# Layer B's fillers tied to earlier score products, doses by half pair, and the norm's broadcast behind its row copy

## The chip, the core and the metric

One core of one Trainium2 chip runs the whole program. Its engines work side by side, each through its own list of instructions in a fixed order: PE (TensorE) multiplies matrices, DVE (VectorE) and ACT (ScalarE) work on whole tiles and read what PE has written, POOL (GpSimd) works on tiles in the large on-chip memory, and SP issues most DMA transfers. The metric is the device time of one launch in microseconds (us), taken as the median of several runs; less is better.

## What is computed

A trunk of two decoder layers on one sequence of 512 positions with 1024 channels, in float32. Layer A is attention with compressed, selected and windowed branches, and is not touched here. Layer B reads shared keys and values through three groups of dilated windows, which are merged by their softmax sums, beside an attention over 256 memory rows. Each layer ends in a squared-ReLU MLP.

```python
DIL_PATTERNS = ((128, 1), (512, 4), (2048, 16))
...
for gi, (window, dil) in enumerate(DIL_PATTERNS):
    ...
    s = jnp.einsum('bhqd,bhqkd->bhqk', q_b[:, gi], k_g).astype(jnp.float32) * scale
    s = jnp.where(valid, s, NEG)
    lse = jax.nn.logsumexp(s, axis=-1, keepdims=True)
    p = jnp.exp(s - lse)
    outs.append(jnp.einsum('bhqk,bhqkd->bhqd', p.astype(v.dtype), v_g))
    lses.append(lse)
wts = jax.nn.softmax(jnp.stack(lses), axis=0).astype(v.dtype)
return jnp.sum(jnp.stack(outs) * wts, axis=0)
...
x = x + jnp.concatenate([o_main, o_mem], axis=-1) @ b_w_out[i]
x = x + squared_relu_mlp(rmsnorm(x, mlp_norm[layer]), w_up[layer], w_down[layer])
```

## The kernel before

The eight slots (heads) of layer B are taken in four *slot pairs*, sp = 0 to 3; the two slots of a pair lie in the two halves of the 128 partitions, so that their products use the two halves of the PE array side by side. The queries of pair 0 are projected before the attention begins. Everything else that PE has to do in this layer is *filler*: the query projections of pairs 1 to 3 (`proj_b`), that of the memory queries (`mem_q`), and the first part of the output projection (`outpart`). Each filler step is one `mm3` (lines 267 to 272): three products, high times high, high times low, low times high, which together stand for one product in float32.

`attn_b` makes eight items for a pair: two slots s, two window halves w (w = 0 is the near window, w = 1 the two dilated ones) and two halves ih of the query blocks. `scores` (products at line 762) runs once for both slots of an item pair and fills the two banks of the pool `ps`; one such call is called a *score group* here, and there are 16. `soft` masks the scores on DVE (line 737), takes exponentials on ACT (line 226) and, for w = 1, adds the two dilated groups on POOL (line 1635). The `back` of an item transposes the exponentials on PE (lines 1646 and 1655) and copies them on ACT (line 750); when all of a window half are there, `close0` or `close1` multiplies them with the values (line 754). `norm_b` then merges the two halves: sums are transposed and copied to rows (lines 1695 to 1701), a chain of small DVE steps makes the factors (lines 1706 to 1718, 307, 308), they are transposed again (line 1725) and copied to rows (line 1729), and two products spread them over the partitions (*the broadcast*, lines 1733 and 1738), which ACT (line 1735) and DVE (lines 1736, 1739) read. `norm_b` runs as a generator in `side`, one step per item; `NY` and `NZ` are the numbers of steps that it lets pass ahead of line 1725, and between the row copy and the broadcast.

`attend` emits fronts and backs of the items in turn, a back two items behind its front, and after each it lets `side` go one step and `work` (the fillers) as many as a dose says: `RB[seg]`, added up, where `seg` is the pair, or 4 for the memory items. The order in which the engines run this is then set by the framework's scheduler, which moves instructions of the emitted program forward on a modelled time line as far as their inputs, buffers and given dependences allow. `add_manual_dep` gives it a dependence that the data don't have.

PE's results go to banks: `acc` 2 (projections), `ps` 2 (scores), `po` 1 (products with values), and `pt` 2 with one more bank, `px`, that every third tile of `pt` gets. A tile can be written only when what was in its bank has been read. DX is the number of steps by which the transposes of pair 0's queries trail their projection.

Of the kernel before, what the change touches and what calls it, by code (L numbers as in the profile page):

```python
# [44 lines left out]


RA = (2.22, 1.29, 1.62, 1.96)
RB = (1.58, 1.85, 1.29, 2.4, 1.9)


RC = (6.5, 0.6, 0.7)

WK = 0.13
WB = (26, 0)
DX = 12


PA = 13
# [1 line left out]

DELAY = 5

NY, NZ = 6, 2

NW = 11
END, WAIT = object(), object()
# [26 lines left out]
class Work:  # L93


    def __init__(self):
        self.q, self.done = [], set()
# [29 lines left out]
class Item:  # L127


    def __init__(self, front, back, args, seg, need=None):  # L130
        self.front, self.back, self.args, self.seg, self.need = front, back, args, seg, need


def paced(gen, n):
# [4 lines left out]
        next(gen, None)  # L139


def attend(items, work, side, ratios, seen, lag=1):


    late, due = [], 0.0

    def tick(it):
        nonlocal due
        side.step()
        due += ratios[it.seg]  # L150
        while due >= 1.0:
            due -= 1.0
            if work.step() in (END, WAIT):
                due = 0.0

    def back(it):
        it.back(*it.args, it.res)
        tick(it)

    for it in items:  # L160
        if it.need:
            work.need(it.need)
        it.res = it.front(*it.args)
        seen.append(it.seg)
        tick(it)
        late.append(it)
        if len(late) > lag:
            back(late.pop(0))
    for it in late:
        back(it)  # L170
# [10 lines left out]
class K:  # L181
    def __init__(self, ctx, tc, ins, out):
        self.tc, self.nc, self.ins, self.out = tc, tc.nc, ins, out
        ps = lambda n, b: ctx.enter_context(tc.tile_pool(name=n, bufs=b, space=bass.MemoryType.PSUM))
        sb = lambda n, b: ctx.enter_context(tc.tile_pool(name=n, bufs=b))
        self.pacc, self.pS, self.pT, self.pO = ps("acc", 2), ps("ps", 2), ps("pt", 2), ps("po", 1)
        self.px, self.third, self.turns = ps("px", 1), self.pS, 0
        self.one = sb("one", 1)
        self.sb = sb("sb", 1)
        self.dram = ctx.enter_context(tc.tile_pool(name="dram", bufs=1, space=bass.MemoryType.DRAM))  # L190
        self.n = 0
        self.ev = 3
        self.staged = []
        self.sums, self.marks = {}, []
        self.adds, self.far = self.blocks(), 5
        self.lab = "s"

    BUFS = dict(
        act=12, st=3, w=4, qk=8, pt4=4, p2=6, raw=2, tmp=4, sq=1, rb=1, tq=2, qki=2, ki=2, x=8, r1=1, r2=1, r3=1, r4=2, r5=2, r6=3, r7=2, nm=6, su=5, cr=6, c1=2, c2=2, nb=4,
# [67 lines left out]
    def mm3(self, ps, lh, rh, start, stop, again=False):  # L267

        mm = self.nc.tensor.matmul
        mm(ps, lh[0], rh[0], start=start, stop=False, skip_group_check=again)  # L270
        mm(ps, lh[0], rh[1], start=False, stop=False, skip_group_check=again)  # L271
        mm(ps, lh[1], rh[0], start=False, stop=stop, skip_group_check=again)  # L272

# [478 lines left out]
    def pair(self, *a, **k):  # L752

        i = self.nc.tensor.matmul(*a, **k)  # L754
        self.tc.add_manual_dep(
            i.ins, self.turned.ins.name, mybir.DependencyInfo(mybir.DependencyClass.Sync, mybir.DependencyReason.DATA),
            reason="both halves of the array together",
        )

    def together(self, other, *a, **k):  # L760

# [671 lines left out]
    def layer_b(self):  # L1433
# [52 lines left out]
        items = []  # L1486
        for sp in range(4):
            items += self.attn_b(sp, pb[sp], kp[sp], oT, side)
        items += self.mem_items(self.kf1, qm, kk, om, 4, "mem")
        attend(items, work, side, RB, seen, 2)  # L1490
        while side.step() is not END or work.step() is not END:
            pass
        drain(self.outpart(oT + om, 3, 6, ins["w_bo"], None, 3, 3))
# [77 lines left out]
    def attn_b(self, sp, q4, kv, oT, side):  # L1571
# [8 lines left out]
        def scores(w, ih):  # L1580
# [6 lines left out]
            for ii in range(2):  # L1587
                i, n = 2 * ih + ii, sizes[ii]
                blk = slice(i * P, (i + 1) * P)
                for g in range(1 + w):  # L1590
                    for s in range(2):
# [10 lines left out]
                        else:  # L1602
# [2 lines left out]
                                start=True, stop=True,  # L1605
                            )
                o += n
            for s in range(2):
                made[s] = soft(s, w, ih, Sp[s], sizes)

# [74 lines left out]
            side.add(self.norm_b(st0, st1, acc[0], O, oT))  # L1685

        order = [(s, w, ih) for w in range(2) for ih in range(2) for s in range(2)]
        return [Item(front, back, a, sp, sp or None) for a in order]

    def norm_b(self, st0, st1, acc, O1, oT):  # L1690

# [179 lines left out]
```

## Time and profile before

| | us |
|---|---|
| median of three runs | 1251.24 |
| lowest and highest run | 1250.85, 1255.25 |
| the profiled execution | 1249.75 |
| its span, first to last instruction | 1248.0 |
| PE busy in the span | 1223.8 |
| weight loads of PE busy | 1000.9 |
| DVE, ACT, POOL busy | 817.5, 720.2, 336.5 |

The span is that of the profiled execution; 1.75 us of its time lie outside it. The granted clock is the share of its full rate that PE's clock had, and its mean is 0.997 over the span. A row of the view in order of time gives the start, the duration, the engine, the source line, the operation with its result and inputs, the number of instructions merged in it, and in brackets how long the engine stood idle before it and what ended that. Matmuls overlap, so a row's duration is longer than the time to the next start. One product in float32 is two instructions in the trace, so a row of the program's order with one product is x2 there.

### The profile page before, as it was taken

Reading aid. Unit: us, or ns where it says so; the run is one execution under the profiler, and the core shown is the slowest. Engines: PE = TensorE matmul, PEld = TensorE weight load, DVE = VectorE, ACT = ScalarE, POOL = GpSimd, SP = SyncE. Lnnn points to the kernel's source line nnn. Section 1 sums busy time; section 2 is a strip of 40 time slices with the busy share of each in tenths; the row PEclk is TensorE's granted clock in tenths of the full one; section 3 lists DMA queues with packets and bytes.
Section 4 is the critical chain, followed back from the end, with each engine's and each line's share of the span. In section 5 each row is a group of like instructions: output and inputs, shape, how many; then the busy total and the mean of one; then the engine's idle time right before and its main releaser. Section 6 shows DMA issues by size and latency. Waiting matters only on the chain.

```text
span 1248.0 us, 17996 instructions
## 1 busy us (share of the span) xinstructions
PE 1223.8 (98%) x6307; PEld 1000.9 (80%) x6307; DVE 817.5 (66%) x1533; ACT 720.2 (58%) x1579; POOL 336.5 (27%) x452
## 2 busy tenths in 40 slices
PE   9999999999999999999999999988999999999998
PEld 7768877787788888888888888876788888888887
DVE  6857576764567557475589466876767747557466
ACT  6834678873475454463657446666666445364462
POOL 4536874731040000000002786642131000000000
PEclk9999999999999999999999999999999999999999
DMA  7531232442498796896976431211469689697634
GB/s 269 202 105 46 99 105 93 95 118 77 127 287 236 228 271 217 271 245 204 293 206 184 129 96 60 70 39 29 123 193 301 206 269 248 204 290 226 171 106 164
DMA packets 62218, 215.34 MB, mean 173 GB/s; under 512 B 6928, under 2 KB 15312, under 8 KB 61616
## 3 DMA queue, kind: packets, MB, share of 16 engines
q1 hardware_dynamic: 50656, 143.69, 35.4%
q0 software_dynamic: 9728, 35.87, 14.8%
q10 hardware_dynamic: 1744, 34.63, 7.4%
q8 instruction: 50, 0.82, 0.3%
q14 instruction: 40, 0.33, 0.1%
HBM read 208.83 MB, written 72.35 MB: 225 GB/s over the span
## 4 chain that ended last, share of the span: by engine, by line
PE 78%; ACT 4%; DVE 2%; issue 1%; DMA 1%; POOL 1%; ACTq 0%; POOLq 0%; DVEq 0%
PE s_ps L270 13%; PE s_ps L271 13%; PE s_ps L272 13%; PE s_acc L270 6%; PE s_acc L271 6%; PE s_acc L272 6%; PE s_pt L271 3%; PE s_pt L272 3%; PE s_pt L270 3%; PE s_po L754 3%; ACT s_p L226 2%; PE s_ps L762 1%; DVE s_w L265 1%; ACT s_pt L750 1%; DMA s_st<-in_w_mem_dram 1%
## 5 line engine op out<-in xcount | busy, mean ns | idle before, releaser
L265 DVE TENSOR_TENSOR s_w<-s_st,s_w 128x1024 fp32r<-128x1024 f32 (+3 forms) x254 | 293.6, 1161 | 258.9 <-ACT s_w L263 253.5
L263 ACT ACTIVATE s_w<-s_st 128x1024 fp32r<-128x1024 f32 (+4 forms) x260 | 251.8, 971 | 216.3 <-PE s_pt L272 60.0
L270 PE MATMUL s_ps<-s_act,s_w 128*128 128x512 f32 x560 | 218.5, 392 | 0.4 <-DVE s_x L1189 0.3
L271 PE MATMUL s_ps<-s_act,s_w 128*128 128x512 f32 x560 | 218.4, 390 | 0.1
L272 PE MATMUL s_ps<-s_act,s_w 128*128 128x512 f32 x560 | 218.1, 390 | 0.0
L1210 POOL DMA_DIRECT2D sum<-sum x16 | 14.2, 888 | 432.6 <-ACT s_p L226 432.6
L271 PEld LDWEIGHTS s_ps<-s_act,s_w 128*128 128x128 f32 x560 | 105.2, 188 | 22.8 <-issue 0.8
L270 PEld LDWEIGHTS s_ps<-s_act,s_w 128*128 128x128 f32 x560 | 105.0, 188 | 22.9 <-DVE s_x L1189 0.8
L272 PEld LDWEIGHTS s_ps<-s_act,s_w 128*128 128x128 f32 x560 | 105.1, 188 | 21.6
L270 PE MATMUL s_acc<-s_w,s_act 128*128 128x512 f32 (+3 forms) x288 | 101.9, 359 | 1.4 <-ACT s_act L286 0.9
L271 PE MATMUL s_acc<-s_w,s_act 128*128 128x512 f32 (+3 forms) x288 | 101.6, 354 | 0.0
L272 PE MATMUL s_acc<-s_w,s_act 128*128 128x512 f32 (+3 forms) x288 | 100.3, 353 | 0.0
L226 ACT ACTIVATE s_p<-s_ps 128x512 f32<-128x512 f32 x64 | 38.1, 595 | 90.1 <-PE s_ps L272 87.4
L742 POOL TENSOR_SCALAR s_p<-s_p,s_cr,s_ab 128x128 f32<-128x128 f32 (+3 forms) x96 | 62.0, 672 | 58.6 <-DVE s_cr L1099 34.8
L226 ACT ACTIVATE s_p<-s_ps,s_nm 128x256 f32<-128x256 f32 (+3 forms) x128 | 65.7, 527 | 13.9 <-PE s_pt L1117 4.5
L750 ACT ACTIVATE s_pt<-s_pt 128x512 f32<-128x512 f32 (+2 forms) x99 | 51.4, 529 | 27.0 <-PE s_pt L1655 7.3
L270 PEld LDWEIGHTS s_acc<-s_w,s_act 128*128 128x128 f32 x288 | 54.6, 190 | 7.8 <-ACT s_act L286 1.4
L305 ACT ACTIVATE s_qk<-s_p 128x256 fp32r<-128x256 f32 (+1 forms) x96 | 46.9, 489 | 21.2 <-DVE s_p L1220 19.3
L271 PEld LDWEIGHTS s_acc<-s_w,s_act 128*128 128x128 f32 x288 | 54.7, 190 | 4.4 <-issue 0.5
L272 PEld LDWEIGHTS s_acc<-s_w,s_act 128*128 128x128 f32 x288 | 54.5, 190 | 4.1
L308 DVE TENSOR_TENSOR s_qk<-s_p,s_qk 128x256 fp32r<-128x256 f32 (+1 forms) x96 | 50.8, 529 | 0.0
L271 PE MATMUL s_acc<-s_w,s_qk 128*128 128x512 f32 x128 | 49.9, 390 | 0.0
(332 smaller groups left out, 2731.9 us busy)
## 6 DMA issues: line engine op xcount, KB each, us to landing
s_st<-in_w_up_dram SPq DMA_DIRECT2D x64, 512.0 KB, 4.3
s_st<-sum SPq DMA_DIRECT2D x64, 512.0 KB, 6.1
s_st<-in_w_db_dram SPq DMA_DIRECT2D x48, 512.0 KB, 4.5
sum<-in_w_db_dram POOLq DMA_DIRECT2D x16, 1024.0 KB, 14.8
sum<-sum POOLq DMA_DIRECT2D x16, 1024.0 KB, 11.6
s_st<-in_w_bq_dram SPq DMA_DIRECT2D x16, 384.0 KB, 3.5
s_st<-in_w_ag_dram SPq DMA_DIRECT2D x11, 512.0 KB, 3.7
s_w<-in_w_c_dram SPq DMA_DIRECT2D x8, 512.0 KB, 4.8
```

Source lines behind the costliest of these rows:

```text
L226: return lambda *a, **k: self.marks.append(f(*a, **k))
L263: nc.scalar.activation(w[:, 0], st, AF.Copy)
L265: e.tensor_tensor(out=w[:, 1], in0=st, in1=w[:, 0], op=ALU.subtract)
L270: mm(ps, lh[0], rh[0], start=start, stop=False, skip_group_check=again)
L271: mm(ps, lh[0], rh[1], start=False, stop=False, skip_group_check=again)
L272: mm(ps, lh[1], rh[0], start=False, stop=stop, skip_group_check=again)
L305: nc.scalar.activation(dst[:, 0], src, AF.Copy)
L308: nc.vector.tensor_tensor(out=dst[:, 1], in0=src, in1=dst[:, 0], op=ALU.subtract)
L742: self.nc.gpsimd.tensor_scalar(out=p, in0=p, scalar1=c, scalar2=g, op0=ALU.mult, op1=ALU.mult)
L750: self.turned = self.nc.scalar.activation(dst, src, AF.Copy)
L754: i = self.nc.tensor.matmul(*a, **k)
L1210: self.behind(self.nc.gpsimd.dma_start(t[o], x, accum_op=ALU.add, max_dma_last_dim=4096))
```

## The change

Four things, all in layer B. (1) `scores` leaves its last product in a list, `fronts`. After each item, `hold` sets `held` to the last product of the score group two groups back (`HL` = 2), and the first product of the next filler step gets a dependence on it, so a filler emitted after a group is not placed ahead of the group two back. (2) The doses `RB` go by half pair: an item has a `rate`, 2 * sp + w, beside its `seg`, and the memory items have 8; the sums per pair are nearly the same (eight ticks of 2.13 and eight of 2.49 in pair 3 where there were sixteen of 2.4). (3) `NZ` goes from 2 to 0: the broadcast is emitted directly behind the row copy. (4) `DX` goes from 12 to 16.

```diff
-RB = (1.58, 1.85, 1.29, 2.4, 1.9)
+RB = (1.58, 1.58, 1.85, 1.85, 1.3, 1.25, 2.13, 2.49, 1.9)
...
-DX = 12
+DX = 16
+HL = 2
...
-NY, NZ = 6, 2
+NY, NZ = 6, 0
...
-    def __init__(self, front, back, args, seg, need=None):
+    def __init__(self, front, back, args, seg, need=None, rate=None):
         self.front, self.back, self.args, self.seg, self.need = front, back, args, seg, need
+        self.rate = seg if rate is None else rate
...
-def attend(items, work, side, ratios, seen, lag=1):
+def attend(items, work, side, ratios, seen, lag=1, hold=None):
...
         side.step()
-        due += ratios[it.seg]
+        if hold:
+            hold()
+        due += ratios[it.rate]
...
-        mm(ps, lh[0], rh[0], start=start, stop=False, skip_group_check=again)
+        m = mm(ps, lh[0], rh[0], start=start, stop=False, skip_group_check=again)
+        if self.held is not None:
+            self.together_dep(m, self.held, "place of a product")
+            self.held = None
...
+    def hold(self):
+
+        if len(self.fronts) > HL:
+            self.held = self.fronts[-1 - HL]
...
-        items += self.mem_items(self.kf1, qm, kk, om, 4, "mem")
-        attend(items, work, side, RB, seen, 2)
+        items += self.mem_items(self.kf1, qm, kk, om, 8, "mem")
+        attend(items, work, side, RB, seen, 2, self.hold)
+        self.held = None
...
                 o += n
+            self.fronts.append(m)
...
-        return [Item(front, back, a, sp, sp or None) for a in order]
+        return [Item(front, back, a, sp, sp or None, 2 * sp + a[1]) for a in order]
```

`together_dep` is new and calls `add_manual_dep` for its two instructions. The new lines move the code below: in the changed kernel, line 762 for the scores is line 781, 754 is 762, 785 is 804, 1655 is 1676, 1518 is 1538, 1558 is 1578, 1733 and 1738 are 1754 and 1759, 1735 is 1756, 270 to 272 are 275, 279 and 280.

The program's order on PE where pair 1 is normalised while pair 2 is scored, before the change. `s_ps` are scores, `s_pt` transposes and broadcasts (line 1733, 1738), `s_tq` queries of pair 3 on their way, `s_po` products with values:

```order
L762 MATMUL s_ps_8382<-s_qk_8119,s_qk_7706 128x128
L1733 MATMUL s_pt_8431<-s_p_1834_8376,s_ab_6683 128x512
L1738 MATMUL s_pt_8436<-s_p_1834_8376,s_ab_6683 128x512
L1655 MATMUL s_pt_8450<-c_118,s_p_1825_8325 128x128 x2
L1518 MATMUL s_pt_8460<-c_118,s_tq_8403 128x128 x3
L1518 MATMUL s_pt_8511<-c_118,s_tq_8476 128x128 x3
L1558 MATMUL s_pt_8554<-c_118,s_x_6833 128x128
L754 MATMUL s_po_8360<-s_pt_1804_8249,s_x_8132 64x256
```

The same place in the changed kernel, with the 22 rows of one filler (`s_acc_8585`, memory queries) left out but for its ends:

```order
L781 MATMUL s_ps_8394<-s_qk_8119,s_qk_7706 128x128
L275 MATMUL s_acc_8585<-s_w_8577,s_act_7040 128x256
L1754 MATMUL s_pt_8378<-s_p_1834_8376,s_ab_6683 128x512
L1759 MATMUL s_pt_8383<-s_p_1834_8376,s_ab_6683 128x512
L1676 MATMUL s_pt_8439<-c_118,s_p_1824_8319 128x128 x2
L279 MATMUL s_acc_8585<-s_w_8577,s_act_7040 128x256
...
L279 MATMUL s_acc_8585<-s_w_8582,s_act_7047 128x256
L1676 MATMUL s_pt_8450<-c_118,s_p_1825_8325 128x128 x2
L1538 MATMUL s_pt_8460<-c_118,s_tq_8415 128x128 x3
L280 MATMUL s_acc_8585<-s_w_8582,s_act_7047 128x256
L762 MATMUL s_po_8360<-s_pt_1804_8249,s_x_8132 64x256
```

Before, this filler stood ahead of the norm's second transposes (line 1725), and no filler stood in the rows shown; now its 24 products lie between the last scores and the products with values. On ACT at this place, before:

```order
L750 ACTIVATE s_pt_1853_8449<-s_pt_8450 128x256
L226 ACTIVATE s_p_1837_8393,s_stt_7335<-s_ps_8381,s_stt_7335 128x256 x2
L226 ACTIVATE s_p_1838_8399,s_stt_7335<-s_ps_8382,s_stt_7335 128x256 x2
L1735 ACTIVATE s_p_1850_8433<-s_pt_8431 128x512
L1519 ACTIVATE s_qk_8139<-s_pt_8460 128x128
```

And now:

```order
L268 ACTIVATE s_w_8999<-s_st_8997 128x384
L531 ACTIVATE s_r_1860_8482<-s_r_1859_8480,et 128x6
L532 ACTIVATE s_r_1860_8482<-s_r_1860_8482,eps 128x6
L533 ACTIVATE s_r_1860_8482<-s_r_1860_8482 128x6
L1756 ACTIVATE s_p_1836_8380<-s_pt_8378 128x512
L758 ACTIVATE s_pt_1850_8438<-s_pt_8439 128x256
L268 ACTIVATE s_w_9037<-s_st_9035 128x384
L231 ACTIVATE s_p_1841_8405,s_stt_7335<-s_ps_8393,s_stt_7335 128x256 x2
```

The read of the broadcast (line 1735, now 1756) has moved from behind the four exponentials of the last score group to ahead of them, and the split of output weights (`s_w`) now stands around it.

On PE where pair 2 is normalised while pair 3 is scored, before; `s_qki` are memory queries:

```order
L762 MATMUL s_ps_8874<-s_qk_8553,s_qk_8140 128x128
L785 MATMUL s_pt_8924<-idr,s_qki_8866 128x128 x4
L785 MATMUL s_pt_8962<-idr,s_qki_8959 128x128 x4
L1655 MATMUL s_pt_8941<-c_118,s_p_1931_8786 128x128 x2
L1655 MATMUL s_pt_9027<-c_118,s_p_1951_8885 128x128 x2
L658 MATMUL s_pt_8976<-idr,s_qki_8973 128x128 x4
L658 MATMUL s_pt_8989<-idr,s_qki_8986 128x128 x4
L754 MATMUL s_po_8834<-s_pt_1910_8697,s_x_8566 64x256
```

And now, with rows of the products with values and of the output projection (`s_acc_9002`, `s_acc_9040`) left out:

```order
L781 MATMUL s_ps_8865<-s_qk_8553,s_qk_8140 128x128
L804 MATMUL s_pt_8924<-idr,s_qki_8900 128x128 x4
L804 MATMUL s_pt_8962<-idr,s_qki_8959 128x128 x4
L1676 MATMUL s_pt_8935<-c_118,s_p_1925_8769 128x128 x2
L762 MATMUL s_po_8828<-s_pt_1910_8694,s_x_8566 64x256
...
L275 MATMUL s_acc_9040<-s_act_8855,s_w_9037 128x512
L666 MATMUL s_pt_8976<-idr,s_qki_8973 128x128 x4
L279 MATMUL s_acc_9002<-s_act_8855,s_w_8999 128x512
...
L280 MATMUL s_acc_9040<-s_act_8855,s_w_9037 128x512
L666 MATMUL s_pt_8989<-idr,s_qki_8986 128x128 x4
L1676 MATMUL s_pt_9027<-c_118,s_p_1948_8876 128x128 x2
```

The transposes of the last exponentials of pair 3 (`s_pt_9027`) have moved behind the products with values, six products of the output projection and the eight transposes of line 658 (now 666).

More of the change, by code (lines that the diff above doesn't have):

```diff
@@ L196, in __init__ @@
         self.lab = "s"
+        self.held, self.fronts = None, []
     BUFS = dict(
@@ L758, in pair, with together_dep @@
         )
+    def together_dep(self, i, other, why):
+        self.tc.add_manual_dep(
+            i.ins, other.ins.name, mybir.DependencyInfo(mybir.DependencyClass.Sync, mybir.DependencyReason.DATA), reason=why
+        )
+    def hold(self):
+        if len(self.fronts) > HL:
+            self.held = self.fronts[-1 - HL]
     def together(self, other, *a, **k):
```

## The prediction

> **What bounds the kernel now.** I read the page first, then the table of stretches over layer B's attention, then the order of time of PE inside the stretches that were not full, and last ACT, DVE and POOL beside them.
>
> ```profile
> PE 1223.8 (98%) x6307; PEld 1000.9 (80%) x6307; DVE 817.5 (66%) x1533; ACT 720.2 (58%) x1579; POOL 336.5 (27%) x452
> PE 78%; ACT 4%; DVE 2%; issue 1%; DMA 1%; POOL 1%; ACTq 0%; POOLq 0%; DVEq 0%
> ```
>
> PE (the matmul engine) is busy 98% of the span and carries 78% of the chain that ended last, so time is won only where PE stands still, runs slowly or does less. The work on PE is the same before and after, in another order, and the order is the same up to the key and value projection of layer B and again from the last output blocks of that layer on. In the table of stretches that leaves about 691 to 905 us (us from the span's start; the columns are PE, weight loads, DVE, ACT and POOL busy, then the granted clock, the DMA share and GB/s):
>
> ```profile
> 720.00:805.00 85.00, 84.43 (x556) 74.27 (x555) 59.98 (x159) 54.13 (x184) 60.92 (x72) 1.00 0.25 78
> 822.00:831.00 9.00, 5.44 (x41) 3.58 (x43) 6.67 (x24) 6.69 (x29) 5.27 (x7) 1.00 0.00 0
> 858.00:866.00 8.00, 5.13 (x35) 3.23 (x33) 5.51 (x14) 6.81 (x21) 1.45 (x2) 0.79 0.00 0
> ```
>
> PE is nearly full up to 805 us; what it lacks afterwards lies in two places: 822 to 831 us, where slot pair 1 is normalised while pair 2 is scored, and 858 to 866 us, the same one pair later. The first place, PE alone (start, duration, work, and in brackets the idle time before it and who ended it):
>
> ```profile
> 822.96 0.40 PE L1725 MATMUL s_pt<-idr,s_nb 128*8 128x128 f32 x4 [1.03 <-DVE s_nb L308]
> 824.04 0.44 PE L1655 MATMUL s_pt<-c,s_p 128*128 128x128 f32 x2 [0.27 <-POOL s_p L1635]
> 825.50 0.49 PE L1733 MATMUL s_pt<-s_p,s_ab 8*128 8x512 f32 x1
> 827.25 0.55 PE L1518 MATMUL s_pt<-c,s_tq 128*128 128x128 f32 x3 [0.66 <-DVE s_raw L1739]
> 829.47 0.52 PE L1518 MATMUL s_pt<-c,s_tq 128*128 128x128 f32 x3 [1.68 <-ACT s_p L1735]
> 830.14 2.36 PE L754 MATMUL s_po<-s_pt,s_x 128*64 128x256 f32 x16
> ```
>
> The waits are 1.03 + 0.27 + 0.66 + 1.68 = **3.64 us**. The last two are query transposes (L1518) that need a bank of the transpose pool; three banks go round, and two hold the broadcasts of L1733 and L1738 until ACT and DVE have read them. Why that takes so long is seen on ACT and DVE:
>
> ```profile
> 828.26 0.49 ACT L226 ACTIVATE s_p<-s_ps,s_stt 128x256 f32<-128x256 f32 x1
> 828.71 0.62 ACT L1735 ACTIVATE s_p<-s_pt 128x512 f32<-128x512 f32 x1
> 826.52 0.68 DVE L1739 TENSOR_TENSOR s_raw<-s_raw,s_pt 128x512 f32<-128x512 f32 x1
> ```
>
> The read L1735 stands on ACT behind four exponentials of later scores, 3.2 us after its product. The second place:
>
> ```profile
> 855.45 0.44 PE L1655 MATMUL s_pt<-c,s_p 128*128 128x128 f32 x2 [0.32 <-POOL s_p L1635]
> 856.48 1.16 PE L762 MATMUL s_ps<-s_qk,s_qk 64*128 64x128 f32 x14
> 858.88 0.41 PE L1655 MATMUL s_pt<-c,s_p 128*128 128x128 f32 x2 [0.45 <-issue]
> 861.71 0.63 PE L1655 MATMUL s_pt<-c,s_p 128*128 128x128 f32 x2 [2.42 <-POOL s_p L1635]
> 863.50 2.57 PE L754 MATMUL s_po<-s_pt,s_x 128*64 128x256 f32 x16
> ```
>
> Here PE waits 0.32 + 0.45 + 2.42 = **3.19 us** for exponentials of scores it finished only 4.1 us earlier (857.6 to 861.7), and no independent product stands between. Each place is followed by a slow stretch:
>
> ```profile
> 827.60:831.00 3.40, 1.73 (x14) 1.07 (x14) 2.16 (x4) 3.12 (x14) 2.99 (x4) 1.00 0.00 0
> 831.00:834.50 3.50, 3.50 (x22) 2.73 (x16) 3.47 (x9) 2.37 (x8) 3.15 (x3) 0.51 0.02 5
> 858.00:861.70 3.70, 0.84 (x8) 0.49 (x6) 1.95 (x8) 3.57 (x15) 0.72 (x1) 1.00 0.00 0
> 861.70:865.20 3.50, 3.49 (x18) 2.31 (x20) 2.80 (x5) 2.44 (x7) 0.73 (x1) 0.52 0.00 0
> 820.40:823.80 3.40, 2.34 (x19) 1.85 (x18) 2.78 (x16) 1.93 (x9) 1.09 (x3) 1.00 0.24 74
> ```
>
> After 3.4 us with PE busy 1.73 and 0.84, the next 3.5 us ran at 0.51 and 0.52 of the clock; after 2.34 busy it did not drop. Half a clock for 3.5 us loses 1.7 us of work, twice **3.4 us**. [...]
>
> **The change, part by part.** *Removed.* At the first place the new order puts the projection of the memory queries (24 products of 128x256) between the scores and what waits for them, and sets the read of the broadcast on ACT ahead of the exponentials. How long those products take, from the first and the last of the 24:
>
> ```profile
> 818.80 0.39 PE L270 MATMUL s_acc<-s_w,s_act 128*128 128x256 f32 x1
> 821.65 0.28 PE L272 MATMUL s_acc<-s_w,s_act 128*128 128x256 f32 x1
> ```
>
> That is 2.85 us over 23 steps, 0.124 each, so the 22 between are 2.7 us of cover, more than the 1.68 + 0.66 they hide; the 1.03 goes because DVE's eleven steps of the norm now stand in one piece, ahead of the four maskings and the two weight splits that stood among them, while PE has about as much work as before between the row's transposes and theirs. At the second place the products with values (16 rows), six output products and eight transposes stand ahead of the transposes that waited 2.42 us. A group with values at full clock is this row:
>
> ```profile
> 800.16 1.74 PE L754 MATMUL s_po<-s_pt,s_x 128*64 128x256 f32 x16
> ```
>
> 1.7 us of that, six output products (128x512, by the 0.17 us step of 128x384 below 0.23 each, so 1.4) and eight transposes (0.9 by the next row) give 4.0 us of cover against 2.42 + 0.45.
>
> ```profile
> 857.56 0.87 PE L785 MATMUL s_pt<-idr,s_qki 128*128 128x128 f32 x8
> ```
>
> With the waits both half-clock stretches go: 3.64 + 3.19 + 3.4 = **10.2 us** removed.
>
> *What is late next.* I walked the new order with the durations above. First place: DVE then has two weight splits of 1.18 us (the row below; they were done earlier before), four maskings and the norm's five operations in one row, and the scores of pair 3 stand behind the key copy that DVE does after them. I get 0.2 us before the products with values and 0.95 before those scores: 1.15. Bounds: nothing, if DVE is 1 us earlier than I walk it, and 3.6, if it is as late as before. I take 1.1, as the walk has it.
>
> ```profile
> 810.72 2.36 DVE L265 TENSOR_TENSOR s_w<-s_st,s_w 128x1024 fp32r<-128x1024 f32 x2
> ```
>
> Second place: L1733's counterpart comes one score row and no transpose after the row copy on DVE, which took 0.68:
>
> ```profile
> 854.67 0.68 DVE L1729 CAST s_p<-s_pt 8x512 fp32r<-8x512 f32 x1 [0.89 <-PE s_pt L1725]
> ```
>
> So 0.6 us shows there; 0.35 and 0.45 before a transpose of memory queries and before the output products whose low half DVE writes last: 1.4, between 0 and the 3.19 of before.
>
> *The added dependence.* It is of PE on PE, and PE runs its products in order anyway, so it is no wait at run time; it only keeps fillers from being placed ahead of scores. Queued behind a score that waits for its bank is then the filler, and behind that everything on PE. The bank is free when the exponentials have read it:
>
> ```profile
> 812.17 1.14 PE L762 MATMUL s_ps<-s_qk,s_qk 64*128 64x256 f32 x8
> 816.36 0.49 ACT L226 ACTIVATE s_p<-s_ps,s_stt 128x256 f32<-128x256 f32 x1
> ```
>
> From 813.3 to 816.9 is 3.6 us. The shortest stretch between two score groups that I count in the new order is 4.05 us (in pair 2: 15 products of 128x384 at 0.17, nine transposes at 0.14), so the cover is 0.4 us and I cost it at nothing; what it costs without that cover is the slower rival. SP and POOL issue the same DMAs, a few rows exchanged, and DMA stands at 0.00 of its time at both places: nothing.
>
> *Switches.* A product behind another kind of product is later to the next:
>
> ```profile
> 807.35 0.42 PE L270 MATMUL s_acc<-s_w,s_act 128*128 128x384 f32 x1
> 807.61 0.33 PE L271 MATMUL s_acc<-s_w,s_act 128*128 128x384 f32 x1
> 807.78 0.34 PE L272 MATMUL s_acc<-s_w,s_act 128*128 128x384 f32 x1
> ```
>
> 0.26 to the next against 0.17, 0.09 more. Fillers follow something else 58 times before and 67 times after: 9 x 0.09 = 0.8 us. One score group fewer is cut in two:
>
> ```profile
> 816.51 0.48 PE L762 MATMUL s_ps<-s_qk,s_qk 64*128 64x128 f32 x2
> 850.82 1.16 PE L762 MATMUL s_ps<-s_qk,s_qk 64*128 64x128 f32 x16
> ```
>
> A piece of two alone takes 0.48; as an eighth of a whole group 1.16 / 8 = 0.15. That gives back 0.3 to 0.4. Together +0.4, between 0 and twice that.
>
> *The rest of the order* (doses, the later transposes of the first pair) moves products among full stretches; between -0.75 (the two small waits of the rows below) and +1.5 (one more wait like the 1.68). I take +0.5.
>
> ```profile
> 792.78 1.16 PE L762 MATMUL s_ps<-s_qk,s_qk 64*128 64x128 f32 x14 [0.43 <-ACT s_p L226]
> 899.89 0.50 PE L270 MATMUL s_ps<-s_act,s_w 128*128 128x512 f32 x1 [0.32 <-DVE s_x L1189]
> ```
>
> **Sum**: -10.2 + 1.1 + 1.4 + 0.4 + 0.5 = **-6.8 us**. The profiled execution took 1249.75 us (span 1248.0), so 1242.95, rounded to **1243**. The median of the runs shown, 1251.24, lies 1.5 above that execution; against it 1243 is 0.66% less.
>
> **The rivals.** *The waits come back smaller* (DVE's row at the first place, or the 0.6 at the second in one window with others, is enough for one half-clock stretch): -10.2 + 1.7 + 4 of waits + 1 of the rest, about 1246.5. For it: DVE is busy 6.67 of 9 us there. Against: cover of 2.7 and 4.0 us. *The clock is not the gaps' doing* and stays: without the 3.4 us the sum is 1246.4. [...] Against it: both drops begin at the ends of the emptiest windows, and no other window here drops. *The change does nothing that counts*, as the scheduler only exchanges which row waits: 1250. Against: the order at both places has fillers now. *Slower*: held fillers stand behind scores that wait for a bank. Fourteen of the sixteen groups are so protected; wherever a weight split on ACT (2.16 for two) falls among the exponentials, the bank is free 3.6 + 2.2 = 5.8 us after the scores against 4.05 of work, a wait of 1.75:
>
> ```profile
> 809.61 2.16 ACT L263 ACTIVATE s_w<-s_st 128x1024 fp32r<-128x1024 f32 x2
> ```
>
> Fourteen times that is 24.5, and 1249.75 - 10.2 + 24.5 gives 1264. Past six groups that wait so the kernel is slower than before, past ten by over 0.5%. Against it: splits of this size happen once, and before the change the one such wait was the 0.43 above.
>
> **How the numbers follow.** Forecast 0.60 (1238 to 1245), smaller waits 0.20, clock 0.04, nothing 0.09, slower 0.07. About 0.5% is what a measurement of this kernel can tell from no change: below 1245.0 or above 1257.5. Faster is the forecast, 0.60; same is 0.20 + 0.04 + 0.09 = 0.33; slower 0.07. The range goes from 1238 (all 10.2 won, the small waits too, and no new one) to 1251, with the case of nothing in it.
>
> **What would show it.** Right: PE busy to within 1.5 us in the stretch where L1746 to L1759 of pair 1 stand, no stretch under 0.9 of the clock between the key projection and the second MLP, ACT's read of the broadcast within 1 us of its product, and no wait over 1 us before the transposes at the second place. Wrong: a score row that waits for an exponential by more than 0.5 us with a filler right behind it; a clock near 0.5 anywhere in layer B; waits for key copies of pair 3 beyond 1 us; or a PE busy time that grows by over 2 us, which would make switches dearer than 0.09.

## The result, and the profile after

| | before | after |
|---|---|---|
| median of six runs, us | 1250.9 | 1244.98 |
| lowest and highest, us | 1249.88, 1255.25 | 1243.23, 1245.59 |
| span of the profiled execution, us | 1248.0 | 1243.3 |
| mean granted clock over the span | 0.997 | 1.000 |

The ratio is 0.9946, 95% interval 0.9931 to 0.9961: faster by a little over half a per cent. The forecast of 1243.0 is 2 us off and the time lies in its range. The first line of the page of the changed kernel:

```profile
PE 1221.7 (98%) x6307; PEld 998.1 (80%) x6307; DVE 815.7 (66%) x1533; ACT 718.7 (58%) x1579; POOL 341.2 (27%) x452
```

PE does the same 6307 products. The span from the first product of layer B's key projection to the first transpose of its output (found in the order of time of each kernel) holds all of the difference that matters. In the table of stretches, before:

```profile
693.63:902.07 208.44, 200.52 (x1293) 166.62 (x1293) 142.20 (x382) 127.51 (x410) 109.25 (x143) 0.98 0.24 72
```

and after, that stretch and three parts of it:

```profile
693.40:897.47 204.07, 198.06 (x1293) 163.77 (x1294) 140.74 (x382) 126.38 (x410) 114.79 (x145) 1.00 0.24 74
720.00:805.00 85.00, 82.56 (x553) 71.62 (x552) 59.21 (x165) 54.58 (x190) 63.33 (x73) 1.00 0.26 78
817.00:831.00 14.00, 13.57 (x101) 11.09 (x100) 11.63 (x23) 10.54 (x36) 9.92 (x10) 1.00 0.24 67
852.00:866.00 14.00, 12.98 (x94) 9.63 (x92) 11.18 (x25) 10.96 (x34) 4.05 (x5) 1.00 0.12 34
```

The stretch is 4.37 us shorter. PE's idle time in it (length less busy) fell from 7.92 to 6.01, 1.9 us; its busy time fell by 2.46. The slow clock that went is worth 3.0 to 3.4 us of that (see the part on the prediction), so some 0.5 to 0.95 us of other busy time came in. Both places that were empty before are nearly full and at full clock. But 720 to 805 us, where 0.57 us were idle before, now has 2.44 idle. PE at the first place after (start, duration, work, idle time before it and who ended that):

```profile
823.09 0.49 PE L1754 MATMUL s_pt<-s_p,s_ab 8*128 8x512 f32 x1
826.88 0.49 PE L1538 MATMUL s_pt<-c,s_tq 128*128 128x128 f32 x3
827.42 1.73 PE L762 MATMUL s_po<-s_pt,s_x 128*64 128x256 f32 x16
829.09 0.55 PE L1538 MATMUL s_pt<-c,s_tq 128*128 128x128 f32 x3
830.02 0.33 PE L1578 MATMUL s_pt<-c,s_x 128*128 128x128 f32 x1 [0.38 <-ACT s_qk L1541]
834.58 0.70 PE L781 MATMUL s_ps<-s_qk,s_qk 64*128 64x256 f32 x4 [0.26 <-DVE s_qk L1579]
```

and ACT there:

```profile
823.62 0.60 ACT L1756 ACTIVATE s_p<-s_pt 128x512 f32<-128x512 f32 x1 [1.16 <-PE s_pt L1754]
826.84 0.52 ACT L268 ACTIVATE s_w<-s_st 128x384 fp32r<-128x384 f32 x1 [2.23 <-DMA s_st<-in_w_bo_dram]
827.27 0.46 ACT L231 ACTIVATE s_p<-s_ps,s_stt 128x256 f32<-128x256 f32 x1
```

ACT reads the broadcast 0.53 us after its product, and only then comes to a weight conversion that waits for a transfer, and to the exponentials. The query transposes (L1538) wait for nothing. The second place:

```profile
853.62 0.49 PE L1754 MATMUL s_pt<-s_p,s_ab 8*128 8x512 f32 x1
856.79 1.73 PE L762 MATMUL s_po<-s_pt,s_x 128*64 128x256 f32 x16
859.89 0.50 PE L279 MATMUL s_acc<-s_act,s_w 128*128 128x512 f32 x1 [0.40 <-DVE s_act L1766]
861.23 0.40 PE L1676 MATMUL s_pt<-c,s_p 128*128 128x128 f32 x2
```

The products with values stand ahead of the last transposes, which no longer wait. What is new are waits elsewhere:

```profile
713.68 0.44 PE L279 MATMUL s_ps<-s_w,s_act 128*128 128x384 f32 x1 [0.63 <-DVE s_w L270]
740.53 0.55 PE L1538 MATMUL s_pt<-c,s_tq 128*128 128x128 f32 x3 [0.46 <-POOL s_tq L1533]
764.32 0.83 PE L275 MATMUL s_acc<-s_w,s_act 128*128 128x384 f32 x2 [0.51 <-ACT s_w L268]
800.70 0.55 PE L1538 MATMUL s_pt<-c,s_tq 128*128 128x128 f32 x3 [1.28 <-POOL s_tq L1533]
893.02 0.73 PE L275 MATMUL s_ps<-s_act,s_w 128*128 128x512 f32 x2 [0.70 <-ACT s_act L313]
```

Together 3.58 us, at places where the kernel before had none of this size. The runs below say whose they are. The waits at 740 and 764 us stand in hold_only (0.40 each) and not in nz_only, so they come with the dependence; the 0.70 stands in nz_only and not in hold_only, so it comes with the early broadcast; the 1.28 is in neither of the two, but in hold_nz (1.30), which has both. The 0.63 comes and goes (0.88 in nz_only and doses_only, none in hold_nz and z2000).

### The profile page after: what moved, and what is told of

The parts are those of the page before. It is cut to its first block, busy times and chain, and to the rows that moved or that the text cites. A ratio compares the mean times of both kernels' runs of the same rounds, so it can differ in the third digit from the quotient of the medians.

```text
span 1243.3 us, 17996 instructions
## 1 busy us (share of the span) xinstructions
PE 1221.7 (98%) x6307; PEld 998.1 (80%) x6307; DVE 815.7 (66%) x1533; ACT 718.7 (58%) x1579; POOL 341.2 (27%) x452
## 4 chain that ended last, share of the span: by engine, by line
PE 67%; DVE 6%; ACT 5%; DMA 5%; POOL 2%; issue 2%; ACTq 0%; POOLq 0%; DVEq 0%
PE s_ps L275 12%; PE s_ps L279 12%; PE s_ps L280 12%; PE s_acc L275 4%; PE s_acc L280 4%; PE s_acc L279 4%; PE s_pt L280 3%; PE s_pt L275 3%; PE s_pt L279 3%; PE s_po L762 3%; DVE s_w L270 2%; ACT s_p L231 1%; DMA s_st<-in_w_db_dram 1%; ACT s_w L268 1%; PE s_ps L781 1%
```

## The experiments

Every ratio is against the kernel before, run on the same chip. "Stage" is the length of the stretch above in the profiled execution.

| run | what differs | ratio, 95% interval | stage, us |
|---|---|---|---|
| hold_only | before + the dependence | 1.0025, 1.0013 to 1.0037 | 212.67 |
| nz_only | before + NZ = 0 | 1.0012, 1.0003 to 1.0020 | not taken |
| doses_only | before + the doses | 1.0001, 0.9991 to 1.0010 | not taken |
| hold_nz | before + dependence + NZ = 0 | 0.9948, 0.9937 to 0.9960 | 203.49 |
| z2000 | after, NZ = 2 for pair 0 | 0.9978, 0.9968 to 0.9987 | 207.18 |
| z0200 | after, NZ = 2 for pair 1 | 0.9980, 0.9971 to 0.9988 | 208.82 |
| z0020 | after, NZ = 2 for pair 2 | 0.9986, 0.9977 to 0.9994 | 208.97 |
| z0200d | z0200, DVE reads the broadcast | 0.9950, 0.9938 to 0.9963 | 204.31 |
| keep_tr | before + repeated transposes | 1.0035, 1.0022 to 1.0048 | not taken |
| keep_mm | before + repeated products | 1.0037, 1.0024 to 1.0050 | not taken |
| z6000 | after, NZ = 6 for pair 0 | 0.9974, 0.9963 to 0.9984 | 206.57 |
| hl1 | after, HL = 1 | 1.0060, 1.0048 to 1.0072 | not taken |

### One part of the change at a time

Four kernels, each of them the changed one with parts set back.

```diff
 hold_only (against the changed kernel)
-RB = (1.58, 1.58, 1.85, 1.85, 1.3, 1.25, 2.13, 2.49, 1.9)
+RB = (1.58, 1.58, 1.85, 1.85, 1.29, 1.29, 2.4, 2.4, 1.9)
-DX = 16
+DX = 12
-NY, NZ = 6, 0
+NY, NZ = 6, 2
```

> The kernel before with the dependence alone (HL = 2; doses, NZ and DX as before). Theory of the two places: the order has the 24 memory-query products between the last scores and the products with values of pair 2, so the waits of 0.66 and 1.68 us and the half clock of the first place go (about -4 us with 1 us of new waits), while the second place stands as before with its wait of 2.4 us in front of the last transposes of pair 3 and one stretch at half clock: ratio 0.997, some 1247. Rival (the dependence does everything, the rest is ornament): the whole gain, ratio 0.9946, no stretch at half clock left. Rival (the dependence does nothing): 1.000.

Slower than before instead. PE's waits over 2 us in this run:

```profile
803.89 0.70 PE L781 MATMUL s_ps<-s_qk,s_qk 64*128 64x256 f32 x4 [2.45 <-DVE s_qk L1579]
832.06 0.52 PE L1538 MATMUL s_pt<-c,s_tq 128*128 128x128 f32 x3 [2.31 <-ACT s_p L1756]
865.16 0.69 PE L1676 MATMUL s_pt<-c,s_p 128*128 128x128 f32 x2 [2.17 <-POOL s_p L1656]
```

Both old waits are there, in spite of 23 filler products behind the broadcast at the first place, and a third has come at 801 us. ACT shows why the fillers don't help at the first place:

```profile
828.81 0.52 ACT L268 ACTIVATE s_w<-s_st 128x384 fp32r<-128x384 f32 x1 [3.63 <-DMA s_st<-in_w_bo_dram]
...
831.31 0.61 ACT L1756 ACTIVATE s_p<-s_pt 128x512 f32<-128x512 f32 x1
```

The read of a broadcast that PE made at 825.54 stands behind a weight conversion that idles 3.63 us for its transfer, and behind four exponentials: 5.8 us from product to read, against 0.53 in the changed kernel.

```diff
 nz_only (against the kernel before)
-NY, NZ = 6, 2
+NY, NZ = 6, 0
```

> The kernel before with NZ = 0 alone. Theory of the two places: at the second place the products with values and six output products come ahead of the last transposes of pair 3, so the wait of 2.4 us and its half clock go (-4 us); at the first place no filler stands ahead of the norm's second transposes any more, so DVE's chain shows there as a wait of 2 to 4 us and the half clock may stay: between -4 and 0, ratio 0.997 to 1.000. Rival (the dependence does everything): 1.000 with both half clocks. Rival (NZ does everything): 0.9946.

Nothing won. The early broadcast takes the old waits away. At the first place 21 products of the memory queries stand behind it here too, and ACT reads it 0.66 us after its product (824.94 to 825.60); at the second the products with values stand ahead of the last transposes. But with no filler held back PE has none between 817 us and the broadcast, and waits there, for ACT's exponentials and not for DVE's chain as expected. PE and ACT of this run at the first place:

```profile
818.45 0.44 PE L1646 MATMUL s_pt<-c,s_p 128*128 128x128 f32 x2 [0.84 <-ACT s_p L226]
820.79 1.16 PE L762 MATMUL s_ps<-s_qk,s_qk 64*128 64x128 f32 x14 [1.03 <-ACT s_p L226]
824.53 0.48 PE L762 MATMUL s_ps<-s_qk,s_qk 64*128 64x128 f32 x2 [1.43 <-ACT s_p L226]
825.60 0.38 PE L270 MATMUL s_acc<-s_w,s_act 128*128 128x256 f32 x1
825.60 0.66 ACT L1735 ACTIVATE s_p<-s_pt 128x512 f32<-128x512 f32 x1
```

3.30 us where it was 3.64. At the second place the 2.42 is gone and 0.73 and 0.99 have come, and a stretch of 3.4 us at half clock stands at both places as before (a mean clock of 0.65 over 825 to 828 us and 0.78 over 828 to 831, 0.84 over 858 to 861 and 0.60 over 861 to 864).

```diff
 doses_only (against the changed kernel)
-DX = 16
+DX = 12
-HL = 2
+HL = 99
-NY, NZ = 6, 0
+NY, NZ = 6, 2
```

> The kernel before with the doses by half pair alone (the dependence off by HL = 99, NZ and DX as before). Theory: the order at both places is that of before, so both waits and both half clocks stay and the time is within 0.1% of before. Rival (doses spread the fillers over the pair and so shorten the second place): -1 to -3 us, ratio 0.998.

As expected: no difference, with 1.68 and 2.42 us still at the two places.

```diff
 hold_nz (against the changed kernel)
-RB = (1.58, 1.58, 1.85, 1.85, 1.3, 1.25, 2.13, 2.49, 1.9)
+RB = (1.58, 1.58, 1.85, 1.85, 1.29, 1.29, 2.4, 2.4, 1.9)
-DX = 16
+DX = 12
```

> The changed kernel with the doses and DX of before (dependence and NZ = 0 alone). Theory: the orders at both places are those of the changed kernel, so its time to within 0.5 us: ratio 0.9946 to the kernel before (0.994 to 0.996), no half clock in layer B. Rival (doses or DX carry a part): 2 us or more above the changed kernel, 0.9965.

The whole gain: 0.9948 against 0.9946. Doses and DX carry nothing that can be measured; the dependence and the early broadcast give nothing or less each alone, and the gain only together.

### Which norm needs the early broadcast

The changed kernel with NZ by slot pair; the first number is pair 0's.

```diff
 z0200 (z0020, z2000 and z6000 differ in the tuple)
-NY, NZ = 6, 0
+NY, NZ = 6, (0, 2, 0, 0)
-        for _ in range(NZ):
+        for _ in range(NZ[sp]):
```

> The changed kernel, with two rounds put back between the row copy and the broadcast for pair 1's norm alone (the first place); pairs 0, 2 and 3 keep none. Theory A (what decides the first place is ACT's queue: the read of the broadcast, L1756, stands in it behind a weight conversion and the exponentials of a scored group, and the bank that it frees is that of pair 3's query transposes): TensorE again waits 1.5 to 2.5 us for ACT's L1756 ahead of a query transpose, the clock is halved for one window of 3.4 us behind it (1.7 us lost), the second place stays cured: 1246.5 to 1249.5 us, ratio 0.997 to 0.999. Theory B (my prediction's: the 24 memory-query products that the dependence has put there are cover enough): no wait over 0.6 us at the first place, ratio 0.994 to 0.996 as the changed kernel.

0.9980, as theory A says. PE:

```profile
827.54 0.52 PE L1538 MATMUL s_pt<-c,s_tq 128*128 128x128 f32 x3 [1.64 <-ACT s_p L1756]
```

and ACT ahead of it:

```profile
824.56 0.53 ACT L268 ACTIVATE s_w<-s_st 128x384 fp32r<-128x384 f32 x1 [2.51 <-DMA s_st<-in_w_bo_dram]
...
826.79 0.60 ACT L1756 ACTIVATE s_p<-s_pt 128x512 f32<-128x512 f32 x1
```

The wait is back with the 24 products in place, and a half-clock stretch behind it (the 16 products with values take 2.48 us from 828.48, and 1.73 in the changed kernel). Theory B, which is the cover of 2.7 us in the prediction, falls. This run also waits 2.55 us (1.22 + 0.74 + 0.59) at pair 3's norm near 886 us, with a half-clock stretch there (the mean clock over this run's span, 0.997, is that of two such stretches, an estimate); nothing of that was expected. The order on PE is another there: the norm's second transposes (L1746, 882.43) have no product of the output projection between them and the products with values, where the changed kernel has 16 behind its own (878.32). So the 4 us of this run are not the first place's alone.

> The changed kernel, with two rounds put back between the row copy and the broadcast for pair 2's norm alone (the second place). Theory A (at the second place the early broadcast, not the dependence, brings PV's products ahead of the last transposes of pair 3): with the broadcast late the last transposes stand ahead of PV again and TensorE waits about 2.2 us for GpSimd's L1656; one or more halved windows of 3.4 us follow: 2.2 + 1.7 to 5 us more than the changed kernel, 1248 to 1252 us, ratio 0.998 to 1.001, and the first place stays cured. Theory B (the dependence alone is enough there): 0.994 to 0.996.

0.9986, theory A again. PE:

```profile
859.53 0.69 PE L1676 MATMUL s_pt<-c,s_p 128*128 128x128 f32 x2 [2.42 <-POOL s_p L1656]
861.31 1.12 PE L762 MATMUL s_po<-s_pt,s_x 128*64 128x256 f32 x4
```

The last transposes stand ahead of the products with values, and wait for POOL just as long as before the change.

> The changed kernel, with two rounds put back between the row copy and the broadcast for pair 0's norm alone. The kernel with the dependence and two rounds everywhere was 9.5 us slower than the one with none; the two with pair 1 alone and pair 2 alone put back cost about 4.0 and 5.0 us. If the norms' prices add up, pair 0 is worth 1 us or less either way: ratio 0.994 to 0.9965, with the 1.28 us wait for GpSimd's L1533 gone and one of about 2.4 us for VectorE's key copy in its place. Rival: the prices don't add, pair 0's broadcast is worth 3 us or more: 0.997 and above.

The wait came as said, the price not: 0.9978, some 4 us more than the changed kernel where 1 was expected. The stages say the same: pair 0 alone costs 3.1 us, pair 1 4.75, pair 2 4.9, together 12.75, but all of them at once (hold_only, which keeps the old doses) 8.6. The prices don't add up. One reason is seen in the clock (last section): the three runs have five stretches of 3.4 us at half clock between them (mean clocks of 0.999, 0.997 and 0.997 over their spans), hold_only four (0.97 over its stage). That is some 1.5 us of the 4.15, an estimate; the rest stays open.

```diff
 z0200d (against z0200)
-        nc.scalar.activation(cb, pc, AF.Copy)
+        if sp == 1:
+            nc.vector.tensor_copy(cb, pc)
+        else:
+            nc.scalar.activation(cb, pc, AF.Copy)
```

> The kernel with two rounds put back for pair 1's norm, and the read of that norm's first broadcast done by VectorE in place of ScalarE; TensorE's order is the same as without that up to the query transposes of the first place. Theory A (the wait there ends when the broadcast's bank has been read, whoever reads it): VectorE comes to the read behind a weight split that it ends at about 825.96, so the bank is free about 0.7 us earlier than by ScalarE's 827.27 and TensorE waits 0.7 to 1.1 us there instead of 1.64; the clock may stay full; ratio 0.996 to 0.998. Rival (the transposes wait for something else, a half of the probabilities' transposes or the query's rotation): the wait stays at 1.5 us or more under another name; ratio 0.998.

PE and DVE of this run:

```profile
828.66 0.52 PE L1538 MATMUL s_pt<-c,s_tq 128*128 128x128 f32 x3 [0.80 <-DVE s_p L1757]
```

```profile
827.08 0.82 DVE L270 TENSOR_TENSOR s_w<-s_st,s_w 128x384 fp32r<-128x384 f32 x1 [0.16 <-ACT s_w L268]
827.83 0.68 DVE L1757 COPY s_p<-s_pt 128x512 f32<-128x512 f32 x1
```

The wait is 0.80 in place of 1.64, it now ends with DVE's read, the clock stays full (1.00 over the stage), and 0.9950 is the changed kernel's time again. Not all of that is the read's doing: the 2.55 us and the half-clock stretch near pair 3's norm are gone too, as the order there is the changed kernel's again. At the first place itself 0.45 us for DVE's L1760 are new beside the 0.80. So the first place waits for a bank, and what ends the wait is the engine that reads the broadcast out of it.

### Is the slow clock the idle time's doing

The kernel before, with repeats that write the same values again, meant to fill PE's idle time at the two places.

```diff
 keep_tr (against the kernel before)
+                for g in range(3 * (3 if sp == 3 and b == 1 else 0)):
+                    nc.tensor.transpose(pt[:, g % 3, :], kpair(t[:, 2 * (g % 3) : 2 * (g % 3) + 2]), self.idf)
...
+            for j in range(2 * (8 if sp == 3 and ih == 0 and s == 1 else 0)):
+                nc.tensor.transpose(pt[:, j % 2, :], p[:, j % 2 * 256 : j % 2 * 256 + P], self.idf)
```

In keep_mm both calls are `nc.tensor.matmul(..., self.idf, start=True, stop=True)` with the same operands.

> The kernel before, with TensorE's idle time at the two places filled by repeats of transposes that stand there already: pair 3's query transposes of one row block are issued four times (9 more) and two transposes of its last probabilities nine times (16 more); they write the same values again, so nothing else is computed. Theory C (the halved clock follows from the idle itself, and a transpose counts as work): the waits of 1.68 and 2.42 us shrink by about 1 and 2 us of repeated work, and one or both halved windows go: 1.7 to 3.4 us less, ratio 0.997 to 0.999. Rival D (the halved clock does not come from the idle, or a transpose is not counted as work): two halved windows stay, ratio 0.9995 to 1.0015.

> As the kernel with repeated transposes, but the repeats are ordinary products with the identity (no transpose flag), which write the same values. Theory C: at least one halved window goes, ratio 0.997 to 0.999, whatever the repeats with transposes show; if those kept the halved windows and these don't, a transpose is not counted as work by what grants the clock. Rival D (the halving has another cause than the idle): two halved windows stay, 0.9995 to 1.0015. At the second place the order of PV and the last transposes also moves here, so the first place is the clean one.

Both came out slower by 0.35%, which neither theory had: the repeats take 2.1 us at the first place alone and push back what follows. At the second place they fill nothing: waits of 2.05 (keep_tr) and 2.22 us (keep_mm) are left. The clock rows of the two runs, keep_tr first:

```profile
823.10:826.50 3.40, 2.77 (x22) 1.68 (x21) 2.94 (x10) 1.53 (x8) 1.99 (x3) 0.99 0.00 0
826.50:829.90 3.40, 3.11 (x15) 3.06 (x15) 0.81 (x4) 2.62 (x12) 1.46 (x2) 0.50 0.00 0
```

then keep_mm:

```profile
822.50:825.90 3.40, 2.71 (x21) 1.82 (x22) 2.93 (x11) 1.54 (x8) 1.56 (x2) 1.00 0.00 0
825.90:829.30 3.40, 3.40 (x32) 2.98 (x33) 1.64 (x5) 2.88 (x15) 1.68 (x3) 1.00 0.02 5
```

keep_mm has no half clock at the first place and keep_tr has one. That looks like an answer on transposes, but is none: in keep_tr the clock falls at 826.5 us, and its repeats only begin at 827.49:

```profile
827.49 2.13 PE L1520 MATMUL s_pt<-c,s_tq 128*128 128x128 f32 x9
```

What lies ahead of that is the same in both runs. So the pair tells nothing on what kind of work counts. The better evidence on the clock is in the other runs: it is full (1.00) over the whole stage in after, hold_nz and z0200d, whose waits are 1.30 us at most, and has a half-clock stretch at each place at which an old wait came back (hold_only, z0200, z0020, with 0.97, 0.98 and 0.98 over the stage). But a long wait is neither enough nor needed. z6000 has 1.81 us at 799 us and full clock (1.000 over its span); nz_only has half clock at the second place, where no wait is over 0.99 us. And in hold_only the clock falls at 860.9 us, with PE nearly full ahead of it, while the wait of 2.17 us only begins at 863.0:

```profile
858.00:861.00 3.00, 2.90 (x22) 1.99 (x22) 1.32 (x3) 1.34 (x6) 1.45 (x2) 0.99 0.01 3
861.00:864.00 3.00, 1.71 (x10) 1.15 (x9) 2.33 (x10) 2.42 (x9) 0.00 (x0) 0.50 0.00 0
```

So the two go together in most runs, but that the waits by themselves set the clock is not shown.

### Two tries for a faster kernel

> The changed kernel, with six rounds between the row copy and the broadcast for pair 0's norm alone, so that VectorE does that norm's additions and its output split (L1761, L1765, L1766) behind the key copies and the rsqrt steps of pair 2's query chain; pairs 1 to 3 keep none. Theory E (the 1.28 us that TensorE waits for GpSimd's L1533 in the changed kernel come from the norm's work standing ahead of that chain on VectorE, brought there by the early broadcast): the wait at 800 us goes or falls under 0.4, the rest stays: 1243.7 to 1244.3 us, ratio 0.9935 to 0.9945 where the changed kernel gave 0.9946. Rival F (the wait moves: the norm's work then stands ahead of pair 2's next chain or the first score group's maxima): TensorE idles as long up to 815 us, ratio 0.9946 to 0.998.

0.9974, slower than the changed kernel, and theory E falls as put. In the changed kernel DVE comes to the rsqrt step (L535) of pair 2's query chain just behind the norm's output split:

```profile
797.81 1.09 DVE L1766 TENSOR_TENSOR s_act<-s_raw,s_act 128x512 fp32r<-128x512 f32 x1
798.82 0.65 DVE L535 SCALAR_TENSOR_TENSOR s_r<-s_r,et,s_r 128x6 f32<-128x6 f32 x1
```

In z6000 the split is out of the way, and DVE waits for ACT instead, whose step of that chain stands behind two exponentials; PE:

```profile
799.22 0.55 PE L1538 MATMUL s_pt<-c,s_tq 128*128 128x128 f32 x3 [1.81 <-POOL s_tq L1533]
```

```profile
797.30 0.69 DVE L535 SCALAR_TENSOR_TENSOR s_r<-s_r,et,s_r 128x6 f32<-128x6 f32 x1 [1.05 <-ACT s_r L533]
```

The chain is 1.5 us earlier (797.30 against 798.82), but the 1.74 us of products with values that stood ahead of the wait in the changed kernel now stand behind it, and PE comes to the wait 2.0 us earlier. The rest of the 2.5 us by which the stage is longer lies in PE's busy time and wasn't taken apart.

```diff
 hl1 (against the changed kernel)
-HL = 2
+HL = 1
```

> The changed kernel with each filler step tied to the last score product one item back instead of two (HL = 1). Theory G (what the dependence is worth is where the fillers stand: tied closer, they can no longer run ahead, so more of them stand between the norm's transposes, the broadcast and the scores: 25 fillers behind pair 1's norm transposes where the changed kernel has 4): no wait over 0.5 us at the first and second place, clock full, the 1.28 us of pair 2's query chain stays within 0.5; 1242 to 1245 us, ratio 0.993 to 0.996. Rival H (a closer tie delays the projections that the next pair's scores need, so scores wait for query or key copies): new waits of 1 us or more ahead of a pair's first scores, ratio 0.997 to 1.003.

Rival H, and worse than it said: 1.0060. The longest of the new waits:

```profile
840.43 0.33 PE L1578 MATMUL s_pt<-c,s_x 128*128 128x128 f32 x1 [2.59 <-ACT s_qk L1541]
```

Beside it stand waits of 1.45, 1.09, 1.12 and 1.03 us between 734 and 769 us, for a query's squares and copy, a weight split and a query's scaling, and three stretches of 3.4 us at half clock (a mean of 0.94 over 750 to 780 us, 0.94 over 840 to 870 and 0.95 over 870 to 900). No run was measurably faster than the changed kernel.

## Why the prediction was right, and where it was off

- **"3.64 + 3.19 + 3.4 = 10.2 us removed."** Right for the two large waits and for the clock in kind. In place of the 0.32 at 855 us, for POOL, stands another of 0.32 (853.17 in the changed kernel, for ACT's exponential), so 6.5 us of waits went. "Half a clock for 3.5 us loses 1.7 us" is somewhat too much: at half clock a product of 128x256 comes 0.21 us after the one ahead (833.03 and 833.24 in the kernel before), at full 0.12 (836.77 and 836.89); eight transposes take 1.26 (z0020) against 0.87, 16 products with values 3.26 (hold_only) against 1.73. By these steps the two stretches lost about 3.0 us and not 3.4, an estimate. (The second stretch that the prediction reads as 3.4 us with PE busy 0.84 is 3.7 us long.)
- **The cause at the first place**, "24 products ... and sets the read of the broadcast on ACT ahead of the exponentials". The products, whose size the prediction gave, are not the cure alone: hold_only and z0200 have them without the early read and wait 2.31 and 1.64. And it is not they that the dependence adds: nz_only has 21 of them and the early read without it, and neither old wait, but waits 3.30 ahead of the broadcast, where the changed kernel has other fillers. That part the prediction did not name. "More than the 1.68 + 0.66 they hide" was wrong as a sum: the read was not 3.2 us late but as late as ACT's queue made it, 5.8 us in hold_only.
- **The cause at the second place**, products with values ahead of the last transposes: right, and z0020 shows that it is the early broadcast that puts them there; nz_only has the same order at this place without the dependence.
- **"1.1 us" and "1.4 us" of new waits at the places.** Smaller: 0.38 + 0.26 at the first, 0.40 (forecast 0.45) + 0.29 at the second; the 0.6 behind the row copy did not show.
- **"The dependence is no wait at run time", cost nothing.** Right for HL = 2: no score row waits for an exponential by more than 0.32 us. The slower rival, held fillers behind scores that wait for a bank, did not happen. (The shortest stretch, 15 products at 0.17 and nine transposes at 0.14, adds up to 3.81 us and not 4.05, so the cover was 0.2 us and not 0.4.) hl1 shows another price of a closer tie, waits of the next pair's scores and transposes for their inputs, which the prediction did not name.
- **"The rest of the order moves products among full stretches ... I take +0.5"**, between -0.75 and +1.5. This is the step that failed in size: the five waits listed above are 3.58 us, less the 0.43 at 792 us that went. They are not the doses' doing, since hold_nz without them has four of the five. The largest, 1.28 us, hangs on pair 0's norm, whose broadcast comes early as well: with NZ = 2 for that norm (z2000, hold_only) it is not there, but one of 2.45 for the key copies is, and with NZ = 6 (z6000) it is 1.81. What sets it in the end, DVE's or ACT's queue, stays open. I walked the order only at the two places where a wait went, not at the other norms that the same number moves.
- **Switches, +0.4**: 0.95 us of PE's busy time came in if the slow clock was worth 3.4 us, 0.5 if it was worth 3.0.
- **The sum.** Idle -1.9, clock -3.0 to -3.4, busy work +0.5 to +0.95: 4.4 us less in the stage, 4.7 in the span, against 6.8 forecast. The medians are 5.9 apart, since the profiled execution of the kernel before lies 1.15 us under the median of its six runs and that of the changed kernel 0.14 above its own. The forecast was worked out from that one execution, so its 6.8 is to be held against the 4.6 us between the two profiled executions (1249.75 and 1245.12).
- **The rivals.** "The clock is not the gaps' doing" and stays did not come true: with the waits gone the clock is 1.00 in the whole stage, and each run that brought one of the two waits back has a half-clock stretch there, in hold_only one that begins ahead of the wait. The shortest of these waits was 1.64 us (z0200), while a wait of 1.81 us at 799 us (z6000) left the clock at 1.000; what brings a stretch about is not shown. None of the signs of being wrong showed: the score rows' waits, the clock, the key copies of pair 3 (0.26 us) and PE's busy time all stayed within them.

## What to carry to other kernels

Where PE waits for a bank, look up who reads it, and what stands ahead of that read in its engine's queue; independent products covered the wait here only where that read was early too (23 of them left 2.31 us with the read 5.8 us after its product in hold_only, and nothing was left with the read after 0.53 us in the changed kernel). Two changes that give nothing apart can give everything together (1.0025 and 1.0012 here, and 0.9948 with both), so take them out singly and jointly before one is credited. When one number moves a step of every pass of a loop, walk all passes, since the gain at two of them here was partly paid at a third (the 1.28 us that hang on pair 0's norm).

## What was not expected of the hardware

Half-clock stretches began at even distances in two runs. Quarters of a microsecond of the kernel before, where the clock falls and where it comes back:

```profile
831.00:831.25 0.25, 0.25 (x6) 0.19 (x2) 0.25 (x1) 0.00 (x0) 0.25 (x1) 0.70 0.00 0
834.50:834.75 0.25, 0.25 (x4) 0.25 (x3) 0.22 (x2) 0.00 (x0) 0.15 (x1) 0.98 0.00 0
861.75:862.00 0.25, 0.25 (x2) 0.19 (x2) 0.00 (x0) 0.25 (x2) 0.16 (x1) 0.64 0.00 0
865.00:865.25 0.25, 0.25 (x4) 0.07 (x2) 0.25 (x1) 0.23 (x2) 0.00 (x0) 0.54 0.00 0
```

If each is a mix of 1.0 and 0.5, the falls are at 831.10 and 861.82 and the returns at 834.51 and 865.23: both stretches last 3.41 us, and they begin 30.72 us apart, nine times that. In hold_only the clock falls at 833.63 and at 860.94 (worked out in the same way), 27.31 us apart, eight times that. No run shows why. The same gap can come with half clock or without. The wait of 2.45 us for key copies, in z2000:

```profile
799.10:802.50 3.40, 1.37 (x15) 0.76 (x11) 3.37 (x4) 0.99 (x2) 3.24 (x3) 1.00 0.28 77
802.60:806.00 3.40, 3.09 (x11) 2.44 (x12) 2.29 (x14) 1.75 (x7) 1.07 (x3) 0.50 0.00 0
```

and in hold_only:

```profile
800.50:803.90 3.40, 0.95 (x10) 0.59 (x8) 3.37 (x5) 0.82 (x2) 3.24 (x4) 1.00 0.27 77
803.90:807.30 3.40, 3.40 (x21) 3.03 (x22) 1.98 (x12) 2.67 (x12) 1.06 (x2) 1.00 0.01 2
```

has half clock (0.50) behind it in z2000 and full clock (1.00) in hold_only, though the 3.4 us that hold it are the emptier there (PE busy 0.95 against 1.37). What decides stays open: keep_tr's clock fell after 3.4 us with PE busy 2.77, and the kernel before ran on at full clock after 2.34.

Nor does one kernel get the same clock each time. In the 24 executions of the kernel before that were run beside hold_only the mean granted clock lay between 0.990 and 0.999, which at 3.4 us each is about one to seven half-clock stretches (an estimate), and the times between 1248.73 and 1254.92 us. A single profile, with its two stretches, is one draw of these.
